# First mixer of a two-block network: dense projections issued between the delta rule's chunks, two products with the state merged into one

## The chip, the cores and the metric

The kernel runs on 1 core of one Trainium2 chip. The metric is device time in microseconds (us) of that core, as the median of the runs of a kernel. The core has TensorE (PE; its weight loads are listed apart as PEld), VectorE (DVE), ScalarE (ACT), GpSimd (POOL), and SyncE (SP), which issues the transfers.

## The reference, cut to what matters

512 tokens of 1024 features pass through two blocks of two layers each. The change lies in the mixer of the first layer: a retention with 4 heads and a gated delta rule with 4 heads, both fed by one wide projection, each output normalised, gated by `silu` of another projection and sent through one output projection. The delta rule runs over 8 chunks of 64 tokens with a 128x128 state `s` for each head:

```
def step(s, inp):                                   # one chunk, of 8
    u_n, w_n, a_n, qd_n, kt_n, cd_n = inp
    v_new = u_n - jnp.einsum('bhcd,bhdv->bhcv', w_n, s)
    o = jnp.einsum('bhcd,bhdv->bhcv', qd_n, s) + jnp.einsum('bhij,bhjv->bhiv', a_n, v_new)
    s = s * cd_n + jnp.einsum('bhcd,bhcv->bhdv', kt_n, v_new)
    return s, o
...
y_r = _rms(retention_chunkwise(q_r, k_r, v_r)).reshape(b, t, RET_WIDTH)
y_r = y_r * jax.nn.silu(g_r.astype(f32))
y_d = gated_delta_chunkwise(q_d, k_d, v_d, g, beta)
y_d = rms_norm(y_d, out_gain) * jax.nn.silu(g_d.astype(f32).reshape(b, t, GDN_HEADS, GDN_DV))
y = jnp.concatenate([y_r, y_d.reshape(b, t, GDN_WIDTH)], axis=-1).astype(hn.dtype)
return y @ w_out
```

## The kernel before, in words

A dense projection (`proj`) makes 128 features of all 512 tokens: a 512 KB tile of weights `wr` is loaded by SP, ACT splits off its upper part `wh` (L402), DVE the rest `wl` (L403, two instructions of 512 columns), and PE adds 24 products 128x128x512 into one bank `psacc` (L421, L422, L423: three for each of 8 blocks of features). There are three such banks, three banks `pss` for small products and one bank `psr`.

The mixer is `mixer0_body`. After the projections and the short convolution of the delta rule, DVE solves small triangular systems by substitution (L1134, L1140). From the result each head's `D`, `B`, `DT` give `us` and `wT` (L1165 to L1180). Then come the 8 chunks, with the 4 heads inside each chunk. For one head and one chunk, all in float32 (a product of two float32 operands is two instructions in the profile):

- `wT` times the state (L1197), 128 rows of the array by 64 columns; DVE adds `us` and gives `vn` (L1198);
- `kt` times `vn` (L1200), 64 rows by 128 columns: the update of the state;
- `qdT` times the state (L1202), 128 by 64, and `att` times `vn` (L1203), 64 by 64: the output;
- DVE makes the next state `S` (L1210), ACT copies the output into `og` (L1215).

The first chunk has no `wT` and no `qdT` product, the last no `kt` product: 28 + 28 + 28 + 32 = 116 products. In the program's text the retention of four heads follows (projections L421 to L423, scores L1250, values L1255), and then, for n = 0 to 7, the end of each head: POOL squares (L1269), DVE sums (L1270) and scales (L475), POOL takes the power -1/2 (L479), DVE multiplies (L1272), PE transposes into `psr` (L914), a dense projection gives the gate `sg` (L1277, L1278), DVE multiplies both (L1280, L1282) and the product is split in two parts (L408, L409). The output projection `w0_out` closes the mixer.

The order on each engine is not the text's: a scheduler sorts the instructions by its own estimate of when each can start, with the text as priority, and sets the buffers and waits. Each engine then runs its own list strictly in order. That scheduler has already brought the projections and scores of retention forward, to stand beside the substitution and the inverses.

Of the kernel before, what the change touches and what calls it, by code (L numbers as in the profile page):

```python
# [293 lines left out]
# ----------------------------------------------------------------------------  # L294
# the program
# ----------------------------------------------------------------------------


class Prog:
    def __init__(self, tc, I, ctx):  # L300
# [15 lines left out]
        # in the order of their use: the first gain, x's first rows, the first weights  # L316
# [30 lines left out]
    def phase(self, name, psum, **bufs):  # L347
        """the working tiles of one part of the network: 2 KB tiles by tag, and banks of PSUM by tag"""
# [97 lines left out]
    def mac(self, W, X, cols=slice(0, T), tag=None, off=None):  # L446
        """[128 features, tokens] in PSUM; less the offset of the mean"""
# [33 lines left out]
    def tok_sums(self, sqs):  # L481
        """column form [128 tokens, 4] of the sum over features of [128, 512] tiles"""
# [8 lines left out]
    def spread(self, rs, ps=None):  # L491
        """[128 tokens, n] -> [128, n*128] in PSUM with every partition alike"""
# [5 lines left out]
    def bcast(self, rs):  # L498
        """[128 tokens, 4] -> [128, 512] with every partition alike"""
# [43 lines left out]
    def before_scale(self):  # L543
        """the part of scale() that need not stand right before its use"""
# [4 lines left out]
    def lagged(self, srcs, X, lag):  # L549
        """(i, product of srcs[i] with X), each behind the next ones' matmuls"""  # L550
# [61 lines left out]
    def lru_body(self, h, pool):  # L612
        nc, I = self.nc, self.I
        # -8 * softplus(-lam), softplus(x) = max(x, 0) + log(1 + exp(-|x|))
# [35 lines left out]
        def decay(n):  # L650
            # by groups of four, so that the tables change seldom
            nonlocal after
            with self.tc.issue_after(last):
                for m in range(n - 4, n):
# [3 lines left out]
                    # 1 - a^2 = -tanh(log a) (1 + a^2)  # L658
# [59 lines left out]

    def total(self, tot, new, eng):
        """a running sum of tiles"""  # L720
# [6 lines left out]
    def out_norm(self, x, src, Y, c, l, s, late=2, out=None):  # L727
        """x <- layernorm(alpha*(x + c * product of src(nb) with Y)), in place; the two parts of it.

        A product takes off first what the mean over the first features amounts to before this, so that  # L730
        mean and mean square may be taken at once. The last blocks come by halves of the tokens, each
        normalised behind the other's products."""
# [33 lines left out]
        def products(cols, tags):  # L766
            """the last blocks; tiles with the sums over all but one feature block and those of the squares, and that block"""
# [14 lines left out]
        def stats(cols, sums):  # L782
            """x less its mean; 1/std, alike on every partition"""
# [53 lines left out]
        # the rest goes on between the first products of what comes next  # L837
# [6 lines left out]
    def swiglu(self, x, X, l, s, out=None, scale=None):  # L844
        """x <- layernorm(alpha*x + 0.5*ffn(x)), in place; the two parts of it. With scale, norm_final
        comes first: X lacks the factor per token that scale() gives"""
# [44 lines left out]

    def mixer0(self, h):
        bufs = dict(e=5, z=4, v=4, q=5, k=4, k2=4, qd=4, r=7, o=4, dm=1, w=4)
# [3 lines left out]
    def b3(self, ap, n=P):  # L897
        """[128, 4] -> [128, 4, n]"""
        return ap.unsqueeze(2).to_broadcast([P, NB, n])
# [4 lines left out]
    def by_token(self, out, x, c):  # L904
        """a factor per token to [128 tokens, 4 times 128 features]"""
# [4 lines left out]
    def trans4(self, src, dst, sl=None):  # L910
        """four 128x128 transposes of a [128, 512] tile"""
# [882 lines left out]
```

## Time and profile before

| what | us |
| --- | --- |
| runs of the kernel before | 3419.01, 3419.9, 3462.51 |
| their median | 3419.9 |
| span of the profiled execution, first to last instruction | 3418.7 |
| PE busy in it | 3343.1 |

The profiled execution's own time is not listed apart from its span; the two lower runs lie 0.3 and 1.2 us above that span. In the rows further down, the start of an instruction and that of the next on PE give its spacing, which is what counts on an engine that runs without a gap; the duration of one is longer, since successive products overlap. A time in square brackets is idle time of that engine just before, and behind the arrow stands what ended it.

### The profile page before, as it was taken

The numbers are of one execution on the slowest core, as the hardware profiler recorded it, in microseconds if no ns is written. First come the engines' busy times: TensorE is split into PE (matmuls) and PEld (weight loads), VectorE is DVE, ScalarE is ACT, GpSimd is POOL, SyncE is SP. The second block draws the span as 40 slices with busy tenths as digits, with TensorE's granted clock in tenths as the row PEclk, the third lists the DMA queues.
The fourth block names the chain that finished last, engine by engine and source line by source line (L and its number), as shares of the span: only waits on it lengthen the run. The fifth ranks groups of instructions, "written<-read, shape, count | busy, mean of one in ns | idle before, by whom it ended". The sixth has DMA issues, their size and how long they took to land.

```text
span 3418.7 us, 41218 instructions
## 1 busy us (share of the span) xinstructions
PE 3343.1 (98%) x15718; PEld 2681.8 (78%) x15718; DVE 1893.4 (55%) x3378; ACT 1388.7 (41%) x2680; POOL 343.0 (10%) x287
## 2 busy tenths in 40 slices
PE   8999999999999999999999999999999999999998
PEld 6776888887788888888867788888888877788887
DVE  7855564658674655344578843335333467863334
ACT  6322442436342443223466642224222356752233
POOL 3101110113110110000200100002000210010002
PEclk9999999999999999999999999999999999999999
DMA  3211223232223223232312222322232312122322
GB/s 119 88 51 48 88 91 100 89 109 68 87 94 97 93 86 99 88 102 85 108 56 65 67 81 85 101 89 90 86 103 92 112 59 78 33 89 86 105 89 78
DMA packets 105685, 293.35 MB, mean 86 GB/s; under 512 B 20752, under 2 KB 35344, under 8 KB 105232
## 3 DMA queue, kind: packets, MB, share of 16 engines
q1 hardware_dynamic: 105488, 290.73, 26.8%
q8 instruction: 123, 2.02, 0.2%
q14 instruction: 74, 0.61, 0.1%
HBM read 280.20 MB, written 2.62 MB: 83 GB/s over the span
## 4 chain that ended last, share of the span: by engine, by line
PE 84%; DVE 8%; issue 3%; ACT 2%; POOL 1%; DMA 0%; SPq 0%; ACTq 0%; DVEq 0%; POOLq 0%
PE psacc L421 15%; PE psacc L422 15%; PE psacc L423 15%; PE pss L421 5%; PE pss L423 4%; PE pss L422 4%; PE pst L421 4%; PE pst L422 4%; PE pst L423 4%; PE pso L421 2%; PE pso L423 2%; PE pso L422 2%; PE pst L1384 1%; DVE wl L403 1%; PE pso L1394 1%
## 5 line engine op out<-in xcount | busy, mean ns | idle before, releaser
L402 ACT ACTIVATE wh<-wr 128x512 fp32r<-128x512 f32 (+1 forms) x1008 | 587.5, 616 | 1301.3 <-PE psacc L422 452.1
L403 DVE TENSOR_TENSOR wl<-wr,wh 128x512 fp32r<-128x512 f32 (+1 forms) x1008 | 671.7, 692 | 653.0 <-ACT wh L402 643.4
L421 PE MATMUL psacc<-xh,wh 128*128 128x512 f32 (+1 forms) x1800 | 711.3, 396 | 10.4 <-ACT wh L402 7.8
L423 PE MATMUL psacc<-xh,wl 128*128 128x512 f32 (+1 forms) x1800 | 708.3, 394 | 10.0 <-DVE wl L403 10.0
L422 PE MATMUL psacc<-xl,wh 128*128 128x512 f32 (+1 forms) x1800 | 709.1, 394 | 2.8 <-DVE xl L523 2.4
L423 PEld LDWEIGHTS psacc<-xh,wl 128*128 128x128 f32 x1800 | 342.1, 190 | 90.8 <-DVE wl L403 13.0
L421 PEld LDWEIGHTS psacc<-xh,wh 128*128 128x128 f32 x1800 | 341.5, 190 | 91.4 <-ACT wh L402 9.6
L422 PEld LDWEIGHTS psacc<-xl,wh 128*128 128x128 f32 x1800 | 341.9, 190 | 80.7 <-DVE xl L523 5.6
L421 PE MATMUL psacc<-ph,wh 128*128 128x512 f32 x775 | 308.3, 398 | 4.6 <-DVE pl L409 2.0
L423 PE MATMUL psacc<-ph,wl 128*128 128x512 f32 x775 | 307.6, 397 | 2.4 <-DVE wl L403 2.4
L422 PE MATMUL psacc<-pl,wh 128*128 128x512 f32 x775 | 306.7, 396 | 0.1
L421 PEld LDWEIGHTS psacc<-ph,wh 128*128 128x128 f32 x775 | 145.8, 188 | 40.6 <-PE pss L423 2.8
L423 PEld LDWEIGHTS psacc<-ph,wl 128*128 128x128 f32 x775 | 145.9, 188 | 36.5 <-DVE wl L403 2.8
L422 PEld LDWEIGHTS psacc<-pl,wh 128*128 128x128 f32 x775 | 145.9, 188 | 33.8 <-DVE pl L409 0.9
L421 PE MATMUL pst<-xh,wh 128*128 128x512 f32 (+1 forms) x408 | 155.8, 384 | 4.2 <-ACT xh L818 4.2
L422 PE MATMUL pst<-xl,wh 128*128 128x512 f32 (+1 forms) x408 | 156.2, 385 | 0.2 <-DVE xl L819 0.2
L423 PE MATMUL pst<-xh,wl 128*128 128x512 f32 (+1 forms) x408 | 155.4, 383 | 0.0
L421 PE MATMUL pss<-xh,wh 128*128 128x512 f32 x392 | 155.1, 396 | 0.0
L422 PE MATMUL pss<-xl,wh 128*128 128x512 f32 x392 | 155.0, 395 | 0.0
L423 PE MATMUL pss<-xh,wl 128*128 128x512 f32 x392 | 155.0, 395 | 0.0
L577 DVE SCALAR_TENSOR_TENSOR cv<-u,vecs,cv 128x510 f32<-128x510 f32 (+1 forms) x176 | 131.1, 749 | 5.2 <-ACT cv L575 2.3
L586 POOL TENSOR_TENSOR cv<-cv,cv 128x512 f32<-128x512 f32 x44 | 57.3, 1302 | 542.7 <-DVE cv L577 517.6
(434 smaller groups left out, 5473.3 us busy)
## 6 DMA issues: line engine op xcount, KB each, us to landing
wr<-wg SPq DMA_DIRECT2D x176, 512.0 KB, 3.5
wr<-wu SPq DMA_DIRECT2D x88, 512.0 KB, 3.5
wr<-we SPq DMA_DIRECT2D x64, 512.0 KB, 3.5
wr<-wd SPq DMA_DIRECT2D x32, 512.0 KB, 3.4
wr<-we SPq DMA_DIRECT2D x64, 192.0 KB, 2.3
wr<-wi SPq DMA_DIRECT2D x22, 512.0 KB, 3.8
wr<-w_ret SPq DMA_DIRECT2D x16, 512.0 KB, 3.6
wr<-wl_in SPq DMA_DIRECT2D x16, 512.0 KB, 3.6
```

Source lines behind the costliest of these rows:

```text
L402: nc.scalar.activation(hi[:, a:b], raw[:, a:b], AF.Copy)
L403: nc.vector.tensor_tensor(lo[:, a:b], raw[:, a:b], hi[:, a:b].bitcast(F32), op=ALU.subtract)
L421: nc.tensor.matmul(ps, wh, xh, start=start, stop=False)
L422: nc.tensor.matmul(ps, wh, xl, start=False, stop=False)
L423: nc.tensor.matmul(ps, wl, xh, start=False, stop=stop)
L577: nc.vector.scalar_tensor_tensor(out=e[:, s:], in0=u[:, : T - s], scalar=self.v(f"fcw{l}{2 - s}", ch), in1=e[:, s:], op0=ALU.mult, op1=ALU ...
L586: nc.gpsimd.tensor_tensor(gate[:], gate[:], val[:], op=ALU.mult)
L1384: nc.tensor.transpose(pt[:, qb * P : (qb + 1) * P], t[:, kb * P - k0 : (kb + 1) * P - k0], self.ident)
L1394: nc.tensor.matmul(acc[0:64, q], v[:, kb, 0:64], lo[:, q], start=False, stop=False)
```

## The change

1. The `wT` and `qdT` of a head lie in one tile `wq` of 1024 columns, with the 64 + 64 columns of a chunk next to each other (their order changes from chunk to chunk). One product 128x128 (L1308) replaces the two of 64 columns. The half of the bank that `vn` is not made from is the start of the output, and the product with `att` (L1310) adds onto it, now ahead of the product with `kt` (L1314).
2. In the text, the retention of heads 0 to 2 stands ahead of the inverses. That of head 3, the first five gates and the ends of the four retention heads form a list `dense()`, of which one piece is issued behind each chunk. Three more gates follow the chunks, then the ends of the four delta heads.
3. A gate is made apart from the end of its head: `gate(n)` and `finish(n)`.
4. The decay table `dm` has no buffer of its own any more but shares those of tag `q`; `vn` has 5 buffers for 6.

The core of the diff (the rest drops comments, moves the inverse into a function without other edits, and renames):

```diff
-        bufs = dict(e=5, z=4, v=4, q=5, k=4, k2=4, qd=4, r=7, o=4, dm=1, w=4)
+        bufs = dict(e=5, z=4, v=4, q=5, k=4, k2=4, r=7, o=4, w=4)
...
-            wTs.append(self.copy_act(pw[:], "wT", "k"))
+            nc.scalar.copy(
+                wq[hd][:].rearrange("p (t f j) -> p t f j", t=NB, f=4)[:, :, 0:4:3, :],
+                pw[:].rearrange("p (t s j) -> p t s j", t=NB, s=2),
+            )
...
-            dm = self.t("dm", tag="dm")
+            yield
+            dm = self.t("dm", tag="q")
...
+        for hd in range(3):
+            for _ in retention(hd):
+                pass
+        for hd in range(4):
+            inverse(hd)
+        def gate(n):
+            ps = self.proj(I["w0_ret"][8 + n], X)
+            gates[n] = sg = self.t("sg", tag="e" if n < 4 else "w")
+            nc.vector.tensor_tensor(sg[:], ps[:], bc[:], op=ALU.mult)
+            nc.scalar.activation(sg[:], sg[:], AF.Silu)
...
+        def dense():
+            yield from retention(3)
+            for n in range(5):
+                gate(n)
+                if n < 4:
+                    finish(n)
+                yield
...
-                    nc.tensor.matmul(ps[r, 0:P], wTs[hd][:, qc], S[hd][:], start=True, stop=True)
+                    nc.tensor.matmul(ps[:, 0:P], wq[hd][:, c * P : (c + 1) * P], S[hd][:], start=True, stop=True)
                     nc.vector.tensor_tensor(vna, ps[r, 0:P], us[hd][r, q], op=ALU.add)
-                if c < 7:
-                    nc.tensor.matmul(ps[:, 2 * P : 3 * P], kt[hd][r, q], vna, start=True, stop=True)
-                if c > 0:
-                    nc.tensor.matmul(ps[r, P : 2 * P], qdT[hd][:, qc], S[hd][:], start=True, stop=False)
-                nc.tensor.matmul(ps[r, P : 2 * P], att[hd][r, tb, :], vna, start=c == 0, stop=True)
+                nc.tensor.matmul(
+                    ps[ro, 0:P], att[hd][r, tb, :], vna, start=c == 0, stop=True, skip_group_check=True
+                )
                 if c < 7:
+                    nc.tensor.matmul(ps[:, 2 * P : 3 * P], kt[hd][r, q], vna, start=True, stop=True)
...
+            next(fill, None)
+        for _ in fill:
+            pass
+        for n in range(5, 8):
+            gate(n)
+        for n in range(4, 8):
+            finish(n)
```

Up to the third head's inverse, PE's list is nearly the same as before, since the scheduler had the retention there already. In the chunks it differs. This is PE's list of the kernel before, the second half of one chunk (L1200 `kt`, L1202 `qdT`, L1203 `att`, L1197 `wT`, L421 to L423 dense):

```order
L1200 MATMUL pss_1587<-vn_1588,k_93_495 128x128
L1202 MATMUL pss_1587<-S_1554,qdT_635 64x128
L1203 MATMUL pss_1587<-vn_1588,A_617 64x128
L1197 MATMUL pss_1597<-S_1564,wT_1319 64x128
L423 MATMUL psacc_2372<-xh_156,wl_2366 128x512
L421 MATMUL psacc_2372<-xh_162,wh_2365 128x512
L422 MATMUL psacc_2372<-xl_163,wh_2365 128x512
L1197 MATMUL pss_1607<-S_1574,wT_1358 64x128
```

and this PE's list of the changed kernel in chunk 5 (the sixth), with the end of retention head 1 (L914, four transposes of `or_1545`) in the middle (L1310 `att`, L1314 `kt`, L1308 the merged product):

```order
L1310 MATMUL pss_2277<-vn_2278,A_617 64x128
L1314 MATMUL pss_2277<-vn_2278,k_93_495 128x128
L1310 MATMUL pss_2286<-vn_2287,A_836 64x128
L1314 MATMUL pss_2286<-vn_2287,k_134_714 128x128
L914 MATMUL psr_2267<-cbt,or_1545 128x128 x4
L423 MATMUL psacc_2321<-xh_144,wl_2315 128x512
L1308 MATMUL pss_2304<-S_2221,wq_1166 128x128
L1310 MATMUL pss_2295<-vn_2296,A_1055 64x128
```

Between the two, one product of four is gone, and merged and dense products stand next to each other. Counted over the chunks, the list before has 116 small products, 45 dense ones, 8 transposes and 2 of L1255, with 139 changes of the product's shape, 52 of them between a full 128x128 product and a narrower one; the changed list has 88 small products (28 of L1308), 83 dense ones, 16 transposes and 13 of the retention's products, with 80 changes of shape, 42 of them between full and narrower.

DVE's list in the changed kernel at the same place (L1309 `vn`, L1320 the state, L1256 the gate, L1265, L475 and L1267 the end of the retention head):

```order
L1256 TENSOR_TENSOR sg_2257<-psacc_2232,bc_254 128x512
L1265 TENSOR_REDUCE ro_2260<-sq_2261 128x4
L1309 TENSOR_TENSOR vn_2278<-pss_2277,us_1727 64x128
L475 TENSOR_SCALAR ro_2260<-ro_2260 128x4
L1309 TENSOR_TENSOR vn_2287<-pss_2286,us_1765 64x128
L1267 TENSOR_TENSOR or_1545<-or_1545,ro_2260 128x512
L1320 SCALAR_TENSOR_TENSOR S_2283<-S_2194,cd,pss_2277 128x128
L1320 SCALAR_TENSOR_TENSOR S_2292<-S_2203,cd,pss_2286 128x128
```

The multiplication L1267, which needs the power that POOL takes after L475, now stands ahead of two state updates of the same chunk; the same pattern stands in chunks 6 and 7.

Behind the chunks, PE's list before has the transposes of one `og` (L914) inside each of the last gates, 18 dense products into it:

```order
L422 MATMUL psacc_2531<-xl_169,wh_2524 128x512
L423 MATMUL psacc_2531<-xh_168,wl_2525 128x512
L914 MATMUL psr_2518<-cbt,og_1399 128x128 x4
L421 MATMUL psacc_2531<-xh_174,wh_2524 128x512
L422 MATMUL psacc_2531<-xl_175,wh_2524 128x512
```

and in the changed list the first transposes of an `og` come after 85 dense products that follow the last product with `att`, and all four within 19 products of the output projection:

```order
L423 MATMUL psacc_2595<-xh_180,wl_2589 128x512
L914 MATMUL psr_2630<-cbt,og_1849 128x128 x4
L421 MATMUL psacc_2697<-ph_2184,wh_2690 128x512
L422 MATMUL psacc_2697<-pl_2185,wh_2690 128x512
L423 MATMUL psacc_2697<-ph_2184,wl_2691 128x512
```

On DVE, the four multiplications of `og` stand ahead of the split of the third gate's weights, `wl_2589`. Behind the mixer the lists of both kernels have the same pattern.

## Rows read from the trace of the kernel before

**Rows 1.** The page's part 1: busy us, share, instructions.

```profile
PE 3343.1 (98%) x15718; PEld 2681.8 (78%) x15718; DVE 1893.4 (55%) x3378; ACT 1388.7 (41%) x2680; POOL 343.0 (10%) x287
```

**Rows 2.** Windows: stretch, its length, busy us, TensorE clock, DMA share, GB/s.

```profile
215.00:233.60 18.60, 17.65 (x128) 15.03 (x126) 8.45 (x15) 6.15 (x11) 5.89 (x10) 1.00 0.14 36
233.60:293.60 60.00, 59.97 (x291) 33.70 (x290) 24.79 (x68) 12.80 (x39) 2.39 (x2) 1.00 0.03 10
293.60:341.00 47.40, 39.66 (x179) 30.66 (x179) 31.71 (x50) 15.38 (x27) 13.31 (x11) 1.00 0.20 69
```

**Rows 3.** Timeline of PE within a chunk: start, duration, engine, line, operation, shape, count.

```profile
248.88 0.65 PE L1197 MATMUL pss<-S,wT 128*64 128x128 f32 x4
249.46 0.50 PE L421 MATMUL psacc<-xh,wh 128*128 128x512 f32 x1
249.80 0.40 PE L422 MATMUL psacc<-xl,wh 128*128 128x512 f32 x1
250.12 0.48 PE L1200 MATMUL pss<-vn,k 64*128 64x128 f32 x2
250.54 0.43 PE L1202 MATMUL pss<-S,qdT 128*64 128x128 f32 x2
250.90 0.43 PE L1203 MATMUL pss<-vn,A 64*64 64x128 f32 x2
251.26 0.49 PE L1200 MATMUL pss<-vn,k 64*128 64x128 f32 x2
```

**Rows 4.** Timeline of PE: full float32 products of the inverses, and dense ones.

```profile
225.29 1.16 PE L1175 MATMUL pss<-vb,DT 128*128 128x128 f32 x8
226.29 1.06 PE L1180 MATMUL pss<-DT,kb 128*128 128x128 f32 x8
...
326.03 0.39 PE L421 MATMUL psacc<-xh,wh 128*128 128x512 f32 x1
326.26 0.39 PE L422 MATMUL psacc<-xl,wh 128*128 128x512 f32 x1
```

**Rows 5.** Timeline of the weight loads at the same place as rows 3.

```profile
250.90 0.19 PEld L1203 LDWEIGHTS pss<-vn,A 64*64 64x64 f32 x2 [0.17 <-issue]
```

**Rows 6.** Groups by line and shape, 233.6 to 293.6 us: count, busy, mean ns.

```profile
L1202 PE MATMUL pss<-S,qdT 128*64 128x128 f32 x56 | 12.1, 298 | 0.0
L1203 PE MATMUL pss<-vn,A 64*64 64x128 f32 x56 | 12.0, 294 | 0.0
```

**Rows 7.** Waits of PE, 215 to 345 us: total us, times, longest.

```profile
PE psr L914 <- DVE og L1272: 5.6, 4, 1.6
PE psr L914 <- DVE or L1272: 2.2, 2, 1.4
PE pss L1165 <- DVE DT L1161: 1.0, 1, 1.0
```

**Rows 8.** Timeline of all engines: the ends of two delta heads.

```profile
317.33 0.16 DVE L475 TENSOR_SCALAR ro<-ro 128x4 f32<-128x4 f32 x1
317.40 0.69 DVE L403 TENSOR_TENSOR wl<-wr,wh 128x512 fp32r<-128x512 f32 x1
317.57 1.38 POOL L479 TENSOR_TENSOR ro<-ro,mhalf 128x4 f32<-128x4 f32 x1 [5.46 <-DVE ro L475]
318.93 1.03 POOL L1269 TENSOR_TENSOR sq<-og 128x512 f32<-128x512 f32 x1
318.98 1.52 DVE L1272 TENSOR_TENSOR og<-og,ro 128x512 f32<-128x512 f32 x1 [0.90 <-POOL ro L479]
320.65 0.63 PE L914 MATMUL psr<-cbt,og 128*128 128x128 f32 x4 [1.62 <-DVE og L1272]
...
333.04 0.17 DVE L475 TENSOR_SCALAR ro<-ro 128x4 f32<-128x4 f32 x1
334.70 0.69 DVE L1272 TENSOR_TENSOR og<-og,ro 128x512 f32<-128x512 f32 x1 [0.90 <-POOL ro L479]
335.53 0.63 PE L914 MATMUL psr<-cbt,og 128*128 128x128 f32 x4 [0.79 <-DVE og L1272]
```

More of the change, by code (lines that the diff above doesn't have):

```diff
@@ L1009, in mixer0_body @@
         xscr = self.dram("xscr", (64, 32, 32))
-        kt, qdT, att, lt = [], [], [], []
+        kt, wq, att, lt = [], [], [], []
         nkbe, vbs = [], []
@@ L1091, in head @@
             self.trans4(qd, pd)
-            qdT.append(self.copy_act(pd[:], "qdT", "qd"))
+            t = pool.tile([P, 2 * T], F32, tag="wq", name=self.nm("wq"), bufs=4)
+            wq.append(t)
+            nc.scalar.copy(
+                t[:].rearrange("p (t f j) -> p t f j", t=NB, f=4)[:, :, 1:3, :],
+                pd[:].rearrange("p (t s j) -> p t s j", t=NB, s=2),
+            )
             kt.append(k2)
@@ L1142, in mixer0_body, with inverse @@
             nc.sync.dma_start(xscr[:, :, 16 * c : 16 * c + 16], xb[64 * c : 64 * c + 64])
-        us, wTs = [], []
-        for hd in range(4):
+        us = []
+        def inverse(hd):
             Dm = self.t("D", tag="q")
@@ L1180, in mixer0_body @@
                 nc.tensor.matmul(pw[:, q], nkbe[hd][:, q], DT[:, q], start=True, stop=True)
[L1181 to L1215 removed]
+            nc.scalar.copy(
+                wq[hd][:].rearrange("p (t f j) -> p t f j", t=NB, f=4)[:, :, 0:4:3, :],
+                pw[:].rearrange("p (t s j) -> p t s j", t=NB, s=2),
+            )
         rk_ = ret_consts()
@@ L1223, in mixer0_body, with retention @@
         orr = []
-        for hd in range(4):
+        def retention(hd):
             qk = []
@@ L1262, in mixer0_body, with finish @@
             orr.append(self.copy_act(po[:], "or", "o"))
-        outs = orr + og
-        ys = []
-        for n in range(8):
-            o = outs[n]
+        for hd in range(3):
[3 more added lines that the diff above has]
+            inverse(hd)
+        og = [self.t("og", tag="z") for _ in range(4)]
+        gates, ys = {}, []
+        def gate(n):
[3 more added lines that the diff above has]
+            nc.scalar.activation(sg[:], sg[:], AF.Silu)
+        def finish(n):
+            o, sg = (orr + og)[n], gates[n]
             ro = self.sm(NB, "ro")
@@ L1274, in mixer0_body @@
             self.trans4(o, po)
-            ps = self.proj(I["w0_ret"][8 + n], X)
-            sg = self.t("sg", tag="e")
-            nc.vector.tensor_tensor(sg[:], ps[:], bc[:], op=ALU.mult)
-            nc.scalar.activation(sg[:], sg[:], AF.Silu)
             if n < 4:
@@ L1284, in mixer0_body @@
                 )
-            hi, lo = self.xpair(("v", "k", "k2", "qd")[n // 2])
-            self.split(sg[:], hi[:], lo[:])
-            ys.append((hi, lo))
+            if n // 2 == 3:
+                t = pool.tile([P, 2 * T], F32R, tag="wq", name=self.nm("yq"), bufs=4)
+                hi, lo = t[:, :T], t[:, T:]
+            else:
+                hi, lo = (t[:] for t in self.xpair(("v", "k", "k2")[n // 2]))
+            self.split(sg[:], hi, lo)
+            ys.append((hi, lo))
+        def dense():
[4 more added lines that the diff above has]
+                    finish(n)
+                yield
@@ new lines, in mixer0_body @@
+        fill = dense()
+        S = [None] * 4
+        for c in range(8):
+            tb, s = c // 2, c % 2
+            r, ro = (slice(64 * a, 64 * a + 64) for a in (s, 1 - s))
+            q = slice(tb * P, (tb + 1) * P)
+            for hd in range(4):
+                ps = self.pt()
+                if c == 0:
+                    vn = us[hd]
+                    vna = vn[r, q]
+                else:
+                    vn = pool.tile([P, P], F32, tag="vn", name=self.nm("vn"), bufs=5)
+                    vna = vn[r, :]
+                    nc.tensor.matmul(ps[:, 0:P], wq[hd][:, c * P : (c + 1) * P], S[hd][:], start=True, stop=True)
+                    nc.vector.tensor_tensor(vna, ps[r, 0:P], us[hd][r, q], op=ALU.add)
+                nc.tensor.matmul(
+                    ps[ro, 0:P], att[hd][r, tb, :], vna, start=c == 0, stop=True, skip_group_check=True
+                )
+                if c < 7:
+                    nc.tensor.matmul(ps[:, 2 * P : 3 * P], kt[hd][r, q], vna, start=True, stop=True)
+                    Sn = pool.tile([P, P], F32, tag="S", name=self.nm("S"), bufs=8)
+                    if c == 0:
+                        nc.vector.tensor_copy(Sn[:], ps[:, 2 * P : 3 * P])
+                    else:
+                        cc = s * 16 + tb * 4 + hd
+                        nc.vector.scalar_tensor_tensor(
+                            out=Sn[:], in0=S[hd][:], scalar=cd[:, cc : cc + 1], in1=ps[:, 2 * P : 3 * P],
+                            op0=ALU.mult, op1=ALU.add,
+                        )
+                    S[hd] = Sn
+                nc.scalar.copy(og[hd][r, q], ps[ro, 0:P])
+            next(fill, None)
```

28 lines of the change are left out of this document (removed).

## Prediction, made before the changed kernel ran

> **What bounds the kernel now.** The page's busy shares come first: PE is busy 98% of the span [rows 1], so a change pays only by taking work off PE or by closing a gap in PE's list. The windows by stage come next. From 215 to 341 us, the part that the change rewrites, PE shows three different pictures [rows 2]: in the last inverses 17.65 of 18.60 us are busy; in the chunks 59.97 of 60.00 us, so nothing seems to be won there; behind them 39.66 of 47.40 us, a gap of 7.7 us. The granted clock reads 1.00 in all three, the higher of its two levels (2.4 GHz), and PE ran without long gaps before them, so the clock gives nothing back. The waits of PE name the gaps [rows 7]: four transposes of a delta head for DVE's multiplication (5.6 us), two of a retention head for the same (2.2 us), and one inverse that waits behind such a multiplication (1.0 us): 8.8 us in all. "Busy" in the chunks has to be opened, though. The timeline shows what a product costs by its spacing to the next [rows 3]: the kt product 0.42 us (250.12 to 250.54), qdT 0.36, att 0.36. Two wT products in a row take 0.58 us together, 0.36 for one and 0.22 for the other. Full 128x128 float32 products in a row take 0.25 us each, four of them from 225.29 to 226.29, and a dense product of 512 columns takes 0.23 [rows 4]. So a small product among others of another shape is dearer than a larger one in a stream: the weight loads show 0.17 us of "issue" ahead of a load of another shape [rows 5]. A dense pair between small products takes 0.66 us (249.46 to 250.12) where a stream gives 0.47: 0.1 us at each of its two borders.
>
> **The change part by part.** *The merged product.* The window of the chunks holds 116 small products and 52 borders between full and narrower ones (28 of qdT and 32 of att by the groups [rows 6], two instructions each, eight more att instructions on `us` in the first chunk; the rest by the code). Off its 60.0 us go 45 dense products at 0.233 (10.5), eight transposes, four in 0.4 us (0.8), and two values products (0.5): 48.2 us are left. The prices above give 28 x 0.42 + 88 x 0.36 + 52 x 0.1 = 48.6, so they hold. In the changed list the same is 28 kt x 0.42 = 11.8, 32 att x 0.36 = 11.5, 28 merged products, and 42 borders = 4.2. The merged product has the full shape, so it is no border to the dense product beside it; no row shows it, the nearest are the 0.25 of the full products and the 0.22 of the second wT: I take 0.24, 6.7 us. Sum 34.2, which is 14.0 us less. Bounds: were a merged product as dear as kt, which also has 128 columns of weights (0.42), the sum would be 39.3 and 8.9 us saved. The other end comes from the gap: 139 changes of shape become 80, 59 x 0.17 = 10.0, and 28 products without their gap, 28 x (0.36 - 0.17) = 5.3: 15.3 us saved. I take 14.0, since its prices rebuild the window.
>
> The Trainium skill, "TensorEngine Tiling (Array Packing)", Key Properties, says that a change of tiling mode drains the engine; the 0.17 us of [rows 5] is the one sign of it here. Were the drain the whole price of a change of shape, the saving would be the 15.3 us above; by the spacings it is 14.0. The same list says that different tiles run independently, which speaks against merging; that is a rival below.
>
> *The gaps behind the chunks.* All 8.8 us of waits stand where a head's end is short of dense work. The length of a head's end is in the timeline: from DVE's scaling to the transposes 3.32 us (317.33 to 320.65) where POOL's next squares run beside DVE's multiplication, which then takes 1.52 us, and 2.49 us (333.04 to 335.53) where they do not and it takes 0.69 [rows 8]. In the changed list the first transposes of a delta head have 85 dense products ahead of them, 85 x 0.233 = 19.8 us, so the 5.6 us go. The 1.0 us goes too, as no multiplication stands there any more. The 2.2 us of the retention heads moves into the chunks.
>
> *New waits in the chunks.* The ends of retention heads 1 to 3 stand in chunks 5 to 7, and PE's transposes come before the scheduler's order can cover DVE. In chunk 5, the scaling stands directly behind the first `vn`. From there PE has the rest of one dense product (0.2) and att, kt, att, kt (1.56) until the transposes: 1.8 of the 3.32 us covered, 1.5 us bare. In chunk 6 two more dense products: 1.0 bare. In chunk 7 no kt, but att, dense, att, dense behind the rest of one: about 1.65 covered, and since POOL has no squares to make then, 2.49: 0.8 bare. Sum 3.3. The state updates and `vn` queued behind that multiplication on DVE come in time, as PE reaches them 0.7 us and more after the transposes. Bounds: 0 if the scheduler's list fits, 10.0 if all three lie bare.
>
> *A new wait for weights.* The split of the third late gate's weights (`wl_2589`) stands on DVE behind the ends of all four delta heads. Counted from the last att product, DVE waits for gate 4's projection until 3.1 us (13 x 0.233), makes gate and weights until 5.3 (0.69, twice 0.64, two scalings), then the four powers of 1.38 and the four multiplications of 0.69 run through by 13.6, and gate and half a split by 14.9. PE asks at 61 + 2 products, 14.7. I take 0.5 us; the upper end is four multiplications of 1.52, 3.6 us. The split L403 beside POOL's power keeps its 0.69 [rows 8], so the low end is nearer.
>
> *The tail.* The four heads share one bank `psr`, and the splits of the last one come about 2 us after its transposes. Ten products cover 2.3 us: between 0 and 3, I take 1.0. The merged copies write the same 512 columns on ACT as before: nothing. The decay tables `dm` now wait for buffers of the inverses on SP, and behind them wait weights; the loads land before DVE, the fuller engine there, asks for them: 0, at most 1 us. Another 0.2 for the three banks `pss`.
>
> New waits are 5.0 us against 8.8, so 3.8 us won. **The sum:** 3418.7 - 14.0 - 3.8 = 3400.9 us of span; the median of before is 1.2 above its span: **3402 us**.
>
> **The rivals.** *A, the merged product is no cheaper than kt.* For it: both load 128 columns of weights. Against it: the four products at 0.25. It gives 3419.9 - 8.9 - 3.8 = 3407.
>
> *B, the spreading does nothing.* The scheduler had already filled the chunks with 45 dense products and brought retention forward, so a text in another order may only move the waits. Then the ends of the heads show 8.8 us elsewhere: 3419.9 - 14.0 = 3406.
>
> *C, slower.* The dense products run out in chunks 5 to 7 and at the tail, and PE lies bare for the length of all eight heads' ends. The place is POOL's power with DVE's multiplication behind it. It decides once a head's end costs more than (14.0 + 8.8) / 8 = 2.85 us; at 3.32 each it is 26.6 against 22.8: 3424. For it: a single `psr`, and all of DVE's chunk work queued behind each multiplication. Against it: the 19.8 us of dense work and the end of a retention head that the chunks of before hid.
>
> *D, two 64-column products cost one.* If wT and qdT ran side by side, merging them would save only what the wT product's shape costs, 28 x (0.36 - 0.24) = 3.4, and ten borders, 1.0; with the waits 3.8: 3412. Against it: qdT has a spacing of its own, 0.36 us, in [rows 3], and both write the same 64 output rows. This is the rule on independent tiles of the Trainium skill, "TensorEngine Tiling (Array Packing)", Key Properties.
>
> *E, all new waits vanish:* 3419.9 - 15.3 - 8.8 = 3396.
>
> **How the numbers follow.** Forecast (3398 to 3406) 0.62, A 0.12, B 0.12, C 0.05, D 0.03, E 0.06. The forecast's own bounds are A's 8.9 and 15.3 us saved on products and 2 to 11 us of new waits. From 3397 to 3412 lie the forecast, A, B, a part of D and half of E: about 0.85. Two per cent, about what a measurement of this kernel tells from no change, are 68 us: no case comes near it. Faster by over 2% has 0.01, slower by over 2% 0.01, within 2% 0.98.
>
> **What the profile of the changed kernel would show.** The merged product has a spacing near 0.24 where a full product follows, against 0.42 under A. The waits of PE name DVE's multiplication `or` in chunks 5 to 7 with some 3 us and no `og`; under C they hold over 20 us. A wait for `wl` of at most a few us stands some 15 us after the last chunk. PE's time from 215 us to the first product of the feed-forward part is about 18 us shorter, and from there on both traces agree. What would make it wrong: DVE behind by more than the list shows, so that `vn` and not the transposes holds PE in every chunk, or merged products that wait for the copies of `og` in the three banks.

## The result, and the profile after

The changed kernel takes 3403.0 us as the median of 14 runs (3398.6 to 3412.0). The kernel before, measured beside it, took 3438.8 us as the median of 14 runs (3419.0 to 3463.4), a ratio of 0.990 with a 95% interval of 0.987 to 0.993. The kernel before runs its chunks sometimes at the full and sometimes at half the granted TensorE clock (e7 and e8 below), which puts its runs into two groups, 3419.0 to 3421.5 (6 runs here) and 3432.5 to 3463.4 (8 runs), and the changed kernel has no such second group. Against the lower group, whose trace the prediction used, the change is worth 17 us. The 36 us between the two medians hang on how many of these 14 runs fell into the upper group: beside the experiments fewer than half did, and the median of before was 3420.6, 3424.2 and 3421.5.

The profiled execution of the changed kernel spans 3406.0 us. Part 1 of its page answers [rows 1]: PE is busy for 8.9 us less.

```profile
PE 3334.2 (98%) x15662; PEld 2684.9 (79%) x15662; DVE 1892.5 (56%) x3378; ACT 1387.9 (41%) x2680; POOL 341.0 (10%) x287
```

The windows of the inverses, of the chunks and of what follows (columns as in [rows 2]):

```profile
207.80:232.90 25.10, 24.98 (x172) 21.61 (x172) 9.80 (x15) 9.12 (x16) 5.76 (x12) 1.00 0.22 59
232.90:298.80 65.90, 62.72 (x303) 42.69 (x302) 38.20 (x88) 17.39 (x47) 10.92 (x10) 0.93 0.08 25
298.80:345.00 46.20, 46.20 (x204) 36.90 (x203) 31.32 (x50) 17.39 (x31) 8.25 (x7) 0.98 0.30 91
```

The picture of before is turned round. Behind the chunks PE is now full, where [rows 2] had a gap of 7.7 us; the chunks, which had none, now have 3.2 us of it, and their granted clock reads 0.93 where it read 1.00. The waits of PE from 207 to 345 us (total, times, longest) say the same:

```profile
PE psr L914 <- DVE or L1267: 2.5, 3, 1.2
PE pss L1310 <- DVE vn L1309: 0.7, 1, 0.7
PE pss L1173 <- DVE DT L1169: 0.3, 1, 0.3
```

No `og` and no weight tile `wl` is waited for any more. The group of the merged product in the chunks, to be read beside [rows 6], and places of PE's timeline with the merged product L1308:

```profile
L1308 PE MATMUL pss<-S,wq 128*128 128x128 f32 x56 | 10.6, 292 | 0.0
```

```profile
243.88 0.43 PE L1310 MATMUL pss<-vn,A 64*64 64x128 f32 x2
244.24 0.48 PE L1314 MATMUL pss<-vn,k 64*128 64x128 f32 x2
244.65 0.49 PE L1308 MATMUL pss<-S,wq 128*128 128x128 f32 x2
244.98 1.06 PE L1236 MATMUL psr<-vr,sT 128*128 128x128 f32 x8
...
250.59 0.39 PE L1308 MATMUL pss<-S,wq 128*128 128x128 f32 x2
250.74 0.47 PE L423 MATMUL psacc<-xh,wl 128*128 128x512 f32 x1
...
255.37 0.61 PE L1308 MATMUL pss<-S,wq 128*128 128x128 f32 x4
255.74 0.48 PE L421 MATMUL psacc<-xh,wh 128*128 128x512 f32 x1
```

Behind a `kt` product the merged one takes 0.33 us to the next start, between full products 0.15, and two in a row take 0.37. Summed over all 28 from start to start they take 6.5 us, 0.23 each; the forecast of 0.24 holds. `kt` (0.41) and `att` (0.36) cost what they cost in [rows 3].

What the prediction did not have is in the timeline of all engines in chunk 5, around the transposes of `or`:

```profile
266.10 1.01 POOL L479 TENSOR_TENSOR ro<-ro,mhalf 128x4 f32<-128x4 f32 x1 [20.56 <-DVE ro L475]
...
267.08 1.04 POOL L1264 TENSOR_TENSOR sq<-or 128x512 f32<-128x512 f32 x1
267.14 1.52 DVE L1267 TENSOR_TENSOR or<-or,ro 128x512 f32<-128x512 f32 x1 [0.79 <-POOL ro L479]
...
268.72 0.66 PE L914 MATMUL psr<-cbt,or 128*128 128x128 f32 x4 [1.15 <-DVE or L1267]
...
269.86 0.69 PE L1310 MATMUL pss<-vn,A 64*64 64x128 f32 x2
270.47 0.79 PE L1314 MATMUL pss<-vn,k 64*128 64x128 f32 x2
271.19 0.79 PE L421 MATMUL psacc<-xh,wh 128*128 128x512 f32 x1
...
275.98 0.63 PE L422 MATMUL psacc<-xl,wh 128*128 128x512 f32 x1
276.40 0.46 PE L423 MATMUL psacc<-xh,wl 128*128 128x512 f32 x1
276.70 0.39 PE L421 MATMUL psacc<-xh,wh 128*128 128x512 f32 x1
```

PE waits 1.15 us for the multiplication, and from 269.86 to 276.4 everything on it is slower: `att` takes 0.61 to the next start for 0.36, `kt` 0.72 for 0.41, a dense product 0.42 for 0.23. The granted clock reads 0.50 from 270 to 275 us. The same happens from 296.85 to 300.4, in chunk 7, behind waits of 1.14 and 0.65 us. The windows of PE there (busy, clock, DMA share, GB/s), and what POOL and DVE did ahead of the wait of 1.14 us:

```profile
270.00:275.00 5.00, 5.00 (x13) 0.50 0.00 0
295.00:300.00 5.00, 4.35 (x17) 0.70 0.01 3
```

```profile
293.08 2.48 POOL L1264 TENSOR_TENSOR sq<-og 128x512 f32<-128x512 f32 x2
293.15 1.52 DVE L1267 TENSOR_TENSOR or<-or,ro 128x512 f32<-128x512 f32 x1 [0.79 <-POOL ro L479]
```

What the clock costs can be read from spacings: every product between 269.7 and 276.5 us takes longer than the same product between the same neighbours at the full clock, 3.0 us in sum; from 297.0 to 300.4 it is 1.5. So the lower clock costs 4.5 us in the chunks of this execution.

Since the total also moves with the clock of later parts, the sum is best checked at the stage. The table gives, from PE's timelines, the start of the first inverse product, that of the first `rms` sum of the feed-forward part (L486), and the distance, called the landmark below.

| kernel | first inverse | first L486 | between | clock in the chunks |
| --- | --- | --- | --- | --- |
| before | 207.33 | 382.21 | 174.88 | 1.00 |
| before, e7 | 206.99 | 381.86 | 174.87 | 1.00 |
| before, e8 | 208.35 | 425.62 | 217.27 | 0.52 |
| after | 207.92 | 366.35 | 158.43 | 0.93 |
| after, e10 | 207.72 | 366.17 | 158.45 | 0.93 |
| after, e11 | 208.67 | 365.69 | 157.02 | 0.95 |
| e2 spread only | 208.71 | 399.96 | 191.25 | 0.53 |
| e3 merged product twice | 207.15 | 371.35 | 164.20 | 0.66 to 0.88 in three windows of 5 us |
| e4 early normalisation | 208.12 | 360.63 | 152.51 | 1.00 |
| e5 gate first | 206.74 | 380.87 | 174.13 | 1.00 |
| e6 one late end | 208.60 | 361.55 | 152.95 | 1.00 |
| e9 POOL beside | 208.56 | 361.80 | 153.24 | 1.00 |

In e1 the inverses stand differently, so only its first L486 is compared: 364.38, which is 17.8 us earlier than before.

### The profile page after: what moved, and what is told of

Its sections match the earlier page's. It is cut to its first block, busy times and chain, and to the rows that moved or that the text cites. A ratio compares the mean times of both kernels' runs of the same rounds, so it can differ in the third digit from the quotient of the medians.

```text
span 3406.0 us, 41088 instructions
## 1 busy us (share of the span) xinstructions
PE 3334.2 (98%) x15662; PEld 2684.9 (79%) x15662; DVE 1892.5 (56%) x3378; ACT 1387.9 (41%) x2680; POOL 341.0 (10%) x287
## 4 chain that ended last, share of the span: by engine, by line
PE 85%; DVE 8%; issue 3%; ACT 2%; POOL 1%; DMA 1%; SPq 0%; ACTq 0%; DVEq 0%; POOLq 0%
PE psacc L421 15%; PE psacc L423 15%; PE psacc L422 15%; PE pss L421 5%; PE pss L423 5%; PE pss L422 4%; PE pst L421 4%; PE pst L422 4%; PE pst L423 4%; PE pso L423 2%; PE pso L421 2%; PE pso L422 2%; PE pst L1429 1%; DVE wl L403 1%; DVE cv L602 1%
## 5 line engine op out<-in xcount | busy, mean ns | idle before, releaser
L421 PE MATMUL psacc<-xh,wh 128*128 128x512 f32 (+1 forms) x1800 | 711.9, 396 | 10.6 <-ACT wh L402 7.9
L423 PE MATMUL psacc<-xh,wl 128*128 128x512 f32 (+1 forms) x1800 | 708.3, 394 | 9.6 <-DVE wl L403 9.6
L423 PEld LDWEIGHTS psacc<-xh,wl 128*128 128x128 f32 x1800 | 342.2, 190 | 90.3 <-DVE wl L403 12.7
L421 PEld LDWEIGHTS psacc<-xh,wh 128*128 128x128 f32 x1800 | 341.9, 190 | 89.7 <-ACT wh L402 9.8
L421 PE MATMUL psacc<-ph,wh 128*128 128x512 f32 x759 | 302.7, 399 | 4.6 <-DVE pl L409 2.0
L423 PE MATMUL psacc<-ph,wl 128*128 128x512 f32 x759 | 302.4, 398 | 2.6 <-DVE wl L403 2.6
L421 PEld LDWEIGHTS psacc<-ph,wh 128*128 128x128 f32 x759 | 143.4, 189 | 39.5 <-PE pss L423 2.8
L423 PEld LDWEIGHTS psacc<-ph,wl 128*128 128x128 f32 x759 | 143.3, 189 | 36.0 <-DVE wl L403 3.0
L421 PE MATMUL pst<-xh,wh 128*128 128x512 f32 (+1 forms) x408 | 156.3, 386 | 4.7 <-ACT xh L818 4.7
L423 PE MATMUL pst<-xh,wl 128*128 128x512 f32 (+1 forms) x408 | 156.2, 385 | 0.0
L421 PE MATMUL pss<-xh,wh 128*128 128x512 f32 x392 | 155.2, 396 | 0.0
L423 PE MATMUL pss<-xh,wl 128*128 128x512 f32 x392 | 155.1, 396 | 0.0
```

What stands on the lines that cost most here:

```text
L421: nc.tensor.matmul(ps, wh, xh, start=start, stop=False)
L423: nc.tensor.matmul(ps, wl, xh, start=False, stop=stop)
```

## The experiments

### The parts of the change: e1, e2 and e5

**e1_merge_only** keeps the merged product and takes the spreading away:

```diff
-        for hd in range(3):
+        for hd in range(4):
             for _ in retention(hd):
...
-            yield from retention(3)
-            for n in range(5):
...
+            return
+            yield
...
-        for n in range(5, 8):
-            gate(n)
-        for n in range(4, 8):
-            finish(n)
+        for n in range(8):
+            gate(n)
+            finish(n)
```

> The merged product without the spreading: no dense work is placed in the chunks by the text, the four retentions stand ahead of the inverses, and gates and ends of all eight heads follow the chunks one by one, as before. Theory (the merged product is worth 14.0 us, the spreading 3.8): 3419.9 - 14.0 = 3406 us, the waits for the multiplication of og (some 5 us in four) are back behind the chunks, and a merged product has a spacing of 0.14 to 0.25 us. Rival, the spreading does it all: 3420. Rival A (a merged product as dear as kt): 3411. Rival D (two 64-column products cost one): 3415.

Measured: 10 runs, five at 3400.8 to 3403.4 and five at 3425.5 to 3434.4; ratio to before 0.996 (0.991 to 1.001). The waits of PE in the profiled execution (3402.7 us):

```profile
PE psr L914 <- DVE or L1267: 2.9, 2, 1.6
PE psr L914 <- DVE ro L475: 1.3, 1, 1.3
```

At the full clock this is as fast as the whole change. Its chunks run from the first `att` at 241.52 to the end of the last at 284.85: 43.3 us. Less 39 dense products (9.1), four transposes (0.4) and 0.3 for the one product of an inverse, 33.5 us remain for the small products, where [rows 2] left 48.2: 14.7 us saved. The expected wait for `og` did not come back: the first multiplication of `og` ends at 300.31 and its transposes start at 300.97. Why the scheduler's lists give that here and not in e5 below stays open. 4.2 us of waits stand in place of 8.8. The sum is 14.7 + 4.6 = 19.3 against 17.8 at L486; the 1.5 us between them are not explained.

**e2_spread_only** is the changed kernel with the two 64-column products of before, `kt` ahead of `qdT` and `att` as there, and the buffers that this takes:

```diff
-                    nc.tensor.matmul(ps[:, 0:P], wq[hd][:, c * P : (c + 1) * P], S[hd][:], start=True, stop=True)
+                    nc.tensor.matmul(ps[r, 0:P], wTs[hd][:, qc], S[hd][:], start=True, stop=True)
...
+                if c > 0:
+                    nc.tensor.matmul(ps[r, P : 2 * P], qdT[hd][:, qc], S[hd][:], start=True, stop=False)
```

> The spreading without the merged product: text order of the changed kernel, but wT and qdT as two products of 64 columns, with kt ahead of qdT and att. Theory: 3419.9 - 3.8 = 3416 us, with no wait for og and 2 to 4 us of waits for the retention heads' multiplication within chunks 5 to 7. Rival, the spreading does nothing: 3420. Rival, the spreading does it all: 3403 to 3406. If spreading costs by new waits or a lower granted clock in the chunks: above 3420.

Measured: 10 runs, four at 3410.5 to 3417.2 and six at 3434.9 to 3442.5; ratio 1.000 (0.995 to 1.004). The profiled execution is one of the six; its wait, and the window of its chunks:

```profile
PE psr L914 <- DVE or L1259: 0.7, 1, 0.7
```

```profile
233.60:299.00 65.40, 65.40 (x200) 37.62 (x199) 17.17 (x46) 7.00 (x23) 2.39 (x2) 0.53 0.03 9
```

The four lower runs, which by their time are those at the full clock, have a median of 3412.3, 7 us below the 3419.4 of the lower group of before, and the waits fell by 8.8 - 0.7 = 8.1 (in a trace at half the clock, though, where DVE has more time). The forecast of 3.8 for the spreading was too low. A likely reason is that without the merged product the ends of the retention heads do not lie bare; no trace at the full clock shows it. "The spreading does nothing" falls, at the full clock.

**e5_gate_first** is the kernel before with the projection of a gate ahead of its head's end in the text:

```diff
         for n in range(8):
+            ps = self.proj(I["w0_ret"][8 + n], X)
+            sg = self.t("sg", tag="e")
...
             self.trans4(o, po)
-            ps = self.proj(I["w0_ret"][8 + n], X)
-            sg = self.t("sg", tag="e")
```

> The kernel before with one edit: in the end of a head the text puts the projection of its gate ahead of squares, multiplication and transposes. No merged product, no work placed in the chunks by the text. Theory: the 5.6 us that PE waits for the multiplication of og behind the chunks come from this order alone and fall to under 1.5 us, so the runs at the full clock stand at 3419 - 5 = 3414 us; the merged product without spreading (which has the gates first too) then owes 3414 - 3402 = 12 us to the merged product. Rival: the waits stay or only move, 3419, and the merged product alone is worth 17. In both cases some runs stand 15 to 45 us higher, since the chunks are those of before.

Measured: 3421.2 us, ratio 0.997 (0.992 to 1.002), seven runs at 3417.9 to 3423.1, three at 3442.9 to 3447.4.

```profile
PE psr L914 <- DVE og L1276: 5.9, 4, 1.7
PE psr L914 <- DVE or L1276: 3.3, 2, 1.7
```

My theory for this edit fell: the order of gate and end is worth 0.7 us at the landmark and nothing that the runs can tell; the four waits for `og` are all there.

### The price of a merged product: e3

```diff
                     nc.tensor.matmul(ps[:, 0:P], wq[hd][:, c * P : (c + 1) * P], S[hd][:], start=True, stop=True)
+                    nc.tensor.matmul(ps[:, P : 2 * P], wq[hd][:, c * P : (c + 1) * P], S[hd][:], start=True, stop=True)
```

> The changed kernel with every merged product issued twice, the second into 128 columns of the same bank that nobody reads: 28 products of two instructions more. Theory: a second one costs its spacing of 0.20 to 0.24 us, 5.6 to 6.7 us in all: 3403 + 6 = 3409 us. Rival A: 0.42 each, 11.8: 3415. If the chunks are bound by DVE's chain and not by PE's products: 3403, no change.

The output lacks the part of the state to which `att` should add, presumably because the second product opens a sum of its own in that bank (`start=True`); no run isolates that. Measured: 3413.2 us (3407.5 to 3416.1, 10 runs), 10.2 above the changed kernel; at the landmark 164.20 against 158.43 and 157.02, so 5.8 to 7.2. The fairer of the two is 7.2, since e11 loses as much to the clock as this trace (3.0 us by the spacings); its waits are 3.7 us for 3.2. The pair in PE's timeline:

```profile
245.50 0.49 PE L1309 MATMUL pss<-S,wq 128*128 128x128 f32 x2
245.82 0.39 PE L1308 MATMUL pss<-S,wq 128*128 128x128 f32 x2
246.05 0.39 PE L1309 MATMUL pss<-S,wq 128*128 128x128 f32 x2
246.27 0.39 PE L1236 MATMUL psr<-vr,sT 128*128 128x128 f32 x2
```

The one behind another shape (L1315) takes 0.32, the next two 0.23 and 0.22: 28 x 0.22 = 6.2, inside the 5.8 to 7.2. The times of the runs alone (10.2) would have spoken for A's 0.42; the spacing and the landmark speak against it. The profiled execution is one of the fastest of the ten, 3407.6 us; where the others lose the 3 to 4 us more, no trace shows.

### The waits in the chunks and the clock: e4, e6, e9, e10, e11

**e4_early_norm** divides the end of a head in two. `prep(n)` has the squares, the power and the multiplication, `finish(n)` begins with the transposes:

```diff
...
-            yield from retention(3)
+            for i, _ in enumerate(retention(3)):
+                prep(i)
+                yield
             for n in range(5):
                 gate(n)
+                if n == 0:
+                    prep(3)
                 if n < 4:
                     finish(n)
                 yield
```

> The changed kernel with the squares, power and multiplication of the four retention heads issued in the text three to four chunks earlier than their transposes, so that PE has dense work and chunk work in between; nothing is left out. Theory 1: the waits of PE for the multiplication in chunks 5 to 7 (2.5 us) go, and with them the two stretches of halved granted clock that follow the waits (some 5 us): 3403 - 7 = 3396 us. Theory 2, the stretches of halved clock have nothing to do with the waits: 3403 - 2.5 = 3400.5, with the clock falling in the chunks all the same. Theory 3, DVE's list is what holds PE, and the waits come back as waits for vn or for the state: 3403.

Measured: 3398.9 us (3397.5 to 3401.7, 10 runs), ratio to before 0.990 (0.986 to 0.994). Its only wait, and the window of its chunks:

```profile
PE pss L1320 <- DVE vn L1319: 0.8, 1, 0.8
```

```profile
233.50:294.00 60.50, 59.66 (x307) 41.50 (x307) 33.02 (x81) 18.37 (x50) 5.58 (x5) 1.00 0.08 27
```

The three waits are gone, the clock reads 1.00, and the distance is 152.51: this is the lowest median found, 4.1 us below the changed kernel (e6 and e9 below lie within 2 us of it). Theory 1 gave 3396 and theory 2 3400.5; the time lies between them, the clock speaks for the first.

**e6_late_end_1** puts the normalisation of head 1 alone back behind its gate (the edit is shown against e4):

```diff
-                prep(i)
+                if i != 1:
+                    prep(i)
                 yield
...
+                if n == 1:
+                    prep(1)
```

> The kernel with the early normalisation, except that retention head 1 has its squares, power and multiplication right ahead of its transposes again, as in the changed kernel; heads 0, 2 and 3 stay early. Theory (a wait of PE of a microsecond among the chunks' products is followed by a stretch at half the granted clock): one wait of 1.1 us near 268 us, the granted clock falls to half behind it for some 6 us and nowhere else in the chunks, 1.1 + 3.3: 3399 + 4 = 3403 us. Rival 1, the wait costs only itself: 3400. Rival 2, the clock falls by the mix of products and not by the wait: then it stays full here, or falls at another place.

Measured: 3399.3 us (3396.3 to 3403.1, 4 runs).

```profile
269.63 0.69 DVE L1267 TENSOR_TENSOR or<-or,ro 128x512 f32<-128x512 f32 x1 [0.79 <-POOL ro L479]
...
270.38 0.66 PE L914 MATMUL psr<-cbt,or 128*128 128x128 f32 x4 [0.34 <-DVE or L1267]
```

The wait came out at 0.34 us and not at 1.1, so the run can't tell what a long one does. It tells where the long one comes from: with no squares of the next head on POOL, DVE's multiplication takes 0.69 us for 1.52, and 0.8 us of the wait are gone.

**e9_pool_beside** was to bring that length back with the same list on PE (shown against e6):

```diff
             self.rsq(ro[:], ro[:], 1.0 / P, EPS1)
+            if n == 1:
+                nc.gpsimd.tensor_tensor(self.v3(sq), self.v3(sq), self.b3(ro[:]), op=ALU.mult)
```

> The kernel with the early normalisation but head 1 late, plus one instruction of POOL: behind the power of head 1 it multiplies its finished squares (a tile that nobody reads any more) by the power, so that POOL works on 128x512 while DVE multiplies, as the squares of head 2 do in the changed kernel. PE's list is the same. Theory: DVE's multiplication takes 1.5 us instead of 0.69 and PE's wait near 270 us grows from 0.34 to some 1.2 us; if a wait of that length among these products brings the clock down, the granted clock is halved for some 6 us behind it in this profile, 0.8 + 3.3: 3399 + 4 = 3403 us. Rival 1: the wait costs only itself, 3400, clock 1.00 throughout. Rival 2: POOL's instruction does not slow DVE, 3399.

Measured: 3400.7 us (3397.8 to 3402.8, 10 runs).

```profile
269.89 0.69 DVE L1269 TENSOR_TENSOR or<-or,ro 128x512 f32<-128x512 f32 x1 [0.79 <-POOL ro L479]
269.94 1.55 POOL L1268 TENSOR_TENSOR sq<-sq,ro 128x512 f32<-128x512 f32 x1
270.64 0.66 PE L914 MATMUL psr<-cbt,or 128*128 128x128 f32 x4 [0.33 <-DVE or L1269]
```

Rival 2 holds. DVE started 0.05 us ahead of POOL here and kept its 0.69 us; POOL, which came second, took 1.55 (what this instruction takes alone, no run shows). In the changed kernel POOL started 0.06 us ahead, took 1.04, and DVE took 1.52. So the wait, 0.33 us, was not lengthened, and the question for which the run was made stays open.

**e10_after_again** and **e11_after_again** are the changed kernel, profiled twice more.

> The changed kernel, unchanged, profiled again. Theory: the waits of 1.1 us in chunks 5 and 7 stand where they stood, and the granted clock is halved behind at least one of them; an execution of 3399 us has shorter such stretches than one of 3408. Rival: the halved stretches of the first profile were chance and stand elsewhere in the program, or nowhere.

> The changed kernel, unchanged, profiled once more, with the same expectation: waits in the same places, a halved clock behind at least one of them, and the time higher by what these stretches cost. Rival: no halved clock behind the waits, or at other places.

Measured: 3404.3 and 3401.9 us. Both have the same waits as the first profile (2.5 in three and 0.7). In e10 the clock falls behind both long ones; in e11 it falls behind the first and not behind the second (windows of PE, first e10, then e11):

```profile
270.00:275.00 5.00, 5.00 (x14) 0.50 0.00 0
295.00:300.00 5.00, 4.34 (x16) 0.69 0.01 3
```

```profile
270.00:275.00 5.00, 5.00 (x17) 0.60 0.00 0
295.00:300.00 5.00, 3.79 (x19) 1.00 0.01 3
```

So in three traces of this kernel five of six such places are followed by a reduced clock, at the same points of the list, and in none of e4, e6 and e9, where no wait in the chunks is above 0.85 us, does it fall. The trace of e3 has the same two places, with waits of 1.19 and 1.16 us, and falls behind both: seven of eight. The second stretch costs 158.45 - 157.02 = 1.4 us at the landmark and 1.5 by the spacings. The first costs 3.0 by the spacings. Between e11 and e4 the landmark shows 157.02 - 152.51 = 4.5, of which the waits are (2.5 + 0.7) - 0.8 = 2.4; the 2.1 that remain are less than 3.0, so e4's products must cost 0.9 more elsewhere. Chance stretches anywhere in the program fall as a rival. That the wait by itself brings the clock down is not shown: e11 has a wait of 1.13 us without it, and e4 changed the order of the products as well. Two things speak against the wait as the whole cause: the waits of 1.35 to 1.62 us behind the chunks of the kernel before, among dense products, are followed by no fall, and in e2 above and e8 below the clock falls at the end of the first chunk with no wait just ahead of it (in e8 the last one ends 15 us earlier, in e2 the inverses show none).

### The second group of the kernel before: e7, e8, e12

> The kernel before, unchanged, profiled again. Its runs stand in two groups, at 3415 to 3424 and at 3432 to 3467 us. If this execution is one of the upper group: theory, the granted clock is halved within the chunks (233 to 294 us) and the whole difference lies there; rival, the lower clock lies in the feed-forward parts or the second block. If it is one of the lower group, its chunks read 1.00 and it tells nothing more.

> The kernel before, unchanged, profiled once more, with the same expectation: an execution of the upper group has its lower clock in the chunks (233 to 294 us) and loses its 15 to 45 us there; rival, it loses them elsewhere.

e7 took 3418.3 us, and its chunks read 1.00. e8 took 3461.4 us. Its window of the chunks, and its timeline at the start of the chunks and behind their end; below them the place of L1255 in the trace of before at the full clock:

```profile
234.60:336.00 101.40, 101.40 (x291) 53.19 (x291) 25.65 (x68) 13.03 (x41) 2.39 (x2) 0.52 0.02 6
```

```profile
237.34 0.43 PE L1203 MATMUL pss<-us,A 64*64 64x128 f32 x2
237.69 0.50 PE L1197 MATMUL pss<-S,wT 128*64 128x128 f32 x2
238.13 1.22 PE L1255 MATMUL psr<-vr,sT 128*128 128x128 f32 x4
239.28 0.69 PE L1197 MATMUL pss<-S,wT 128*64 128x128 f32 x2
...
340.04 0.53 PE L422 MATMUL psacc<-xl,wh 128*128 128x512 f32 x1
340.41 0.40 PE L423 MATMUL psacc<-xh,wl 128*128 128x512 f32 x1
```

```profile
237.04 0.71 PE L1255 MATMUL psr<-vr,sT 128*128 128x128 f32 x4
```

After eight small products in a row the clock falls to 0.50, with PE busy throughout, and comes back only in the stream of dense products behind the chunks, at 340 us. The ninth takes 0.44 us to the next start for 0.36, and the four instructions of L1255 behind it 1.22 us, where the kernel before with the full clock has 0.71. The list is the same as in e7. The distance is 217.27 against 174.87: 42.4 us, where the two times differ by 43.0. So in this execution nearly the whole loss lies in the chunks; the other runs of the upper group have no trace. Of the 71 runs of the kernel before that were measured beside the others, 29 lie above 3430 us.

**e12_merge_only_again** profiles e1 once more.

> The kernel with the merged product but without spreading, profiled again. Half of its runs stand at 3401 to 3403, half at 3425 to 3434. If this execution is one of the upper half: theory, the clock is halved in the chunks, as in the kernel before, and the dense work of its chunks is too little to bring it back; rival, it is halved at another place. If it is one of the lower half, the chunks read 1.00.

Measured: 3434.4 us, 32 above the first profile of e1, with the clock down from the first chunk on:

```profile
241.40:305.00 63.60, 63.60 (x193) 40.43 (x191) 19.77 (x57) 9.13 (x30) 2.39 (x2) 0.53 0.03 9
```

Neither part of the change alone keeps the clock: 5 of 10 runs of e1 and 6 of 10 of e2 lie in an upper group of their own, against none of the 14 runs of the whole change and of its two further ones, and none of the 34 of e3, e4, e6 and e9, which have both parts too. The order of `att` ahead of `kt`, which e1 keeps and e2 takes back, and the change of buffers were not run by themselves.

## Why the prediction was right, and where it was not

The median, 3403.0, is 1 us from the forecast, and the change is faster by less than two per cent, as forecast. That it is so near is partly luck: the new waits came out 1.8 us lower than forecast, and the clock took 3.0 to 4.5 us that the forecast did not have. Step by step:

- **The merged product, -14.0: right.** e1 shows 14.7 in its window (17.8 - 4.6 = 13.2 at L486). From e4, 174.88 - 152.51 = 22.4 at the landmark; less the 8.8 of gaps, plus the 0.8 of its wait, 14.4. The spacing of 0.24 stood for a mixture of 0.15 to 0.33. A falls by e3, D by e1. Between the 14.0 by spacings and the 15.3 by the gaps of the weight loads these figures do not decide.
- **The gaps, -8.8: right.** None of the waits for `og` is left, nor the 1.0 us within the inverses; the 0.3 us that the trace shows stand ahead of the first of them.
- **New waits in chunks 5 to 7, 3.3: right in sum** (2.5 and 0.7) **and by luck**; 0 + 0 for `wl` and the tail, for which 0.5 and 1.0 stood. The transposes wait 1.15, 0.24 and 1.14 us in the three chunks, for a forecast of 1.5, 1.0 and 0.8. From DVE's scaling to the transposes it was 2.9 us in each and not 3.32, with 1.0 us for POOL's power in place of 1.38. In chunk 7 the prediction took the shorter row of [rows 8], "since POOL has no squares to make then"; POOL squares `og` there, and DVE's multiplication takes 1.52 us. The prediction had `vn` come in time; in chunk 7 PE waits 0.65 us for it. The bounds of the new waits, 2 to 11 us in all, do not follow from those of the parts (0 to 10.0, up to 3.6, 0 to 3).
- **"The clock gives nothing back": wrong.** This is the step that failed, in two ways. In the changed kernel the clock falls behind the waits and takes 3.0 (e11) to 4.5 us (the first profile and e10). In the kernel before, one of the three runs shown was 3462.51, and the prediction passed it over; by its time it was an execution of the second group. The clock is what makes the median of before 3438.8 and the gain by medians twice the 18 us that were forecast.
- **The sum at the stage:** with e1's 14.7, 174.88 - 14.7 - 8.8 + 3.2 + 4.5 = 159.1, where 158.43 and 158.45 were measured; for e11, with 3.0 of clock, 157.6 and 157.02. Some 0.6 us stay unexplained. Behind the stage the traces do not agree as forecast: from L486 to the end before takes 3036.5 us, the three traces of the changed kernel 3039.7, 3036.3 and 3034.3. And the step from span to time, for which 1.2 us stood, is 1.8 to 1.9 in the runs of both kernels: the sum would have been 3402.7.
- **B falls** as far as the spreading alone gains 7 us at the full clock (e2). On top of the merged product it gains nothing there (e1 3402, after 3403): what it wins behind the chunks it loses to waits and clock within them. Its worth is that the clock holds through most of the chunks. That no run with both parts lies in an upper group, and about half of those with one do, is shown; which property of the list holds it (fewer narrow products, more dense ones among them, or where they stand in the first chunk) is not.
- **C and E did not happen.** E's 3396 is 3 us below what e4 reaches by an edit that the change lacks.

## What to carry to other kernels

Price small products by their spacing among their neighbours, not by their columns; a product merged to the full shape saves the price of the second one and a change of shape as well. Where runs of the kernel before disagree by more than a per cent, get the profile of the slow one first: here e8 lost 42 us in the chunks, more than twice the 18 us of the forecast. And place the normalisation of a head well ahead of its transposes: in seven of eight places a wait of more than a microsecond among small products was followed by 1.5 to 3 us lost in granted clock, though the wait is not shown to be the cause.

## What the hardware did unexpectedly

- A PE that is busy 100% of the time can lose its clock: in e8 101.4 of 101.4 us are busy at a mean granted clock of 0.52, from the ninth small product of the chunks on, and another execution of the same list (e7) keeps it. At half the clock small products are not twice as dear: in the changed kernel's rows above it is 0.61 for 0.36, 0.72 for 0.41 and, for a dense one, 0.42 for 0.23.
- Of a DVE and a POOL instruction on 128x512 operands that start within 0.06 us of each other, the first runs at its own pace and the second takes longer: POOL first, 1.04 and DVE 1.52; DVE first, 0.69 and POOL 1.55. What the latter takes alone no run shows, but the squares that POOL starts at 294.08 us in the changed kernel, while DVE still multiplies, take 1.49 for 1.04. The Trainium skill, "SBUF — State Buffer", Who interferes with whom, says that the order of issue decides which of the two is blocked; the traces agree.
